# Neighbourhood attention two heads at a time, their score products alternating between the two row halves of the array

## The chip, the cores and the metric

The kernel runs on one core of a Trainium2 chip. The metric is the device time of one execution in microseconds (us); lower is better. The core has five engines that run side by side, each through its own instructions in order: TensorE (PE in the rows; PEld is its weight load) multiplies, VectorE (DVE), ScalarE (ACT) and GpSimd (POOL) work element by element, SyncE (SP) issues transfers. Products are written to PSUM, which has eight banks of 512 float32 columns on 128 partitions.

## The reference, cut to what matters

Two layers, each with four token mixers in parallel on the same normalised input, merged by gates and projected. Inputs are a context stream and a latent stream of 256 tokens each, 1024 channels. The change touches the second mixer, neighbourhood attention, with 8 heads of 64 channels: a latent token reads the 256 context keys and, of the latent grid, the keys in a window of columns, with a learned bias; a context token reads context keys alone (first layer only, the second layer needs no context output).

```python
s_win = jnp.einsum('bqhd,brkhd->bhqrk', qr, kb).astype(jnp.float32) * scale + bias
s_win = jnp.where(col_mask[:, None, :], s_win, -jnp.inf)
s_ctx = jnp.einsum('bqhd,bkhd->bhqk', qr, kc).astype(jnp.float32) * scale
s = jnp.concatenate([s_win.reshape(B, H, GRID_W, n_win), s_ctx], axis=-1)
p = jax.nn.softmax(s, axis=-1).astype(v.dtype)
```

The first mixer, latent attention, also has 8 heads. In this kernel its queries and keys fill 128 rows for each head; those of neighbourhood attention fill 64.

## The kernel before

**Products.** A float32 product is made of three matmuls on the halves of an exact split (high by high, high by low, low by high); `mm3` (L388) issues them into one PSUM bank. A weight piece of 128 x 1024 is loaded into one of three `raw` buffers, split by ScalarE (L423, the high part) and VectorE (L424, the low part; the rows show it at the helper's line L370) and used by TensorE (`pc`, products with channels on the partitions; `pj`, with tokens on the partitions; `br`, of the branches; `wo`, of the output).

**Order.** The program is written out by cooperating tasks. A task yields a time for which it is left aside, or a condition; `drive` (L302) gives TensorE to the first task in order of priority that can go on, on a clock of its own (`self.clock`) that each product advances by a cost. So TensorE's order is fixed by hand, and the table `WAIT` holds how long a step is left aside in each layer. The order on the other engines is made by the scheduler of the framework. Each engine then waits by semaphores for what it needs.

**Attention.** `unit` (L791) does one head's 128 queries: three matmuls into a bank `sc` of the pool `pa` (four banks, which also hold `y` and, in the first layer, `ada`), the bias added to the latent half of the keys (VectorE), the row maximum (VectorE), the exponential and its row sum (ScalarE), the reciprocal and the scaling (VectorE). It is left aside for `WAIT["probs"]`; then come transposes into a bank `pt` of another pool (two banks), and copies. `attention` (L815) goes over the streams, the two heads of a column tile and the two query tiles, and starts a unit as soon as fewer than `UNITS`, 3, are in flight. `values` (L836) multiplies by the values when the four units of a stream are done. Keys are 256 for a context query tile and 512 for a latent one.

**Around it.** `na` (L988) takes the four column tiles of two heads in turn. Head 0 of a tile lies on partitions 0 to 63 of `qs` and `ks`, head 1 on 64 to 127 (L999). At the same time, at a lower priority, the layer's own stream of projections runs: `na_qk` makes the queries and keys, then `gate_list` makes the four chunks of merge gates (`pj`), which need nothing from the attention; after them it waits for the attention to be done (L1448) and goes on to the branch products. The first layer has 32 units (16 with 256 keys, 16 with 512), the second 16 with 512 keys.

Of the kernel before, what the change touches and what calls it, by code (L numbers as in the profile page):

```python
# [12 lines left out]
AF = mybir.ActivationFunctionType  # L13
ALU = mybir.AluOpType
# [49 lines left out]
# chunks whose products come out with channels on the partitions  # L64
# [52 lines left out]
def _pieces(w, k, n):  # L117
    """[.., rows, cols] as [.., (column block, row block), partition, k, n], flat"""
    b, rows, cols = w.shape
    return w.reshape(b, rows // (k * P), k, P, cols // n, n).transpose(0, 4, 1, 3, 2, 5).reshape(b, -1)  # L120


def _layout(x, c, ctx, c_ctx, ada_w, ada_b, pre_g, post_g, w_in, mla_q_norm, mla_w_uq, mla_kv_norm, mla_w_ukv, na_rpb,
# [76 lines left out]
# how long the static order of the tensor engine leaves a task aside after the step of that name, for layers 0 and 1  # L200
# [7 lines left out]
    "norm_step": (1.25, 0.61),  # L208
    "filt_in": (3.1, 4.0),
    "filt_sin1": (6.0, 15.54),  # L210
# [5 lines left out]
    "filt_dft": (0.1, 0.5),  # L216
    "filt_out": (1.82, 4.9),
    "probs": (5.63, 6.4),
    "probs_out": (1.36, 1.13),
# [6 lines left out]
    "mla_k": (0.8, 0.5),  # L226
    "mla_q": (0.25, 0.5),
    "mla_q_out": (1.7, 1.69),
    "na_in": (2.48, 0.97),
# [16 lines left out]
    "gla_keys": (6.0, 6.0),  # L246
# [5 lines left out]
    "merged_step": (0.48, 0.0),  # L252
# [3 lines left out]
UNITS = (3, 3)  # L256
# [7 lines left out]
class Block:  # L264
    """Emits the program as cooperating tasks. A task yields how long it is to be left aside before its next
    instruction of the tensor engine, or a condition; the driver keeps the tensor engine's
    order: the first task that can go on, by priority."""
# [141 lines left out]
    def piece(self, src, k, n, spare=False):  # L409
        """row blocks of (high, low) parts; spare: in the pool s, not in the weights' own"""  # L410
# [21 lines left out]
    def w_tok(self, l, name, c, n=256):  # L432
        """a column block, as function of the row block"""
        return self.rows([self.w_in(l, name, 2 * c + i, 4, n) for i in range(2)])
# [5 lines left out]
    def h_alloc(self, l, s):  # L440
        """layer 0: both streams side by side, four row blocks to a tile; layer 1: a tile for each stream"""
# [5 lines left out]
    def hT(self, s, kt, a, b, n=1):  # L447
        """n row blocks of a stream; a, b may span both streams in layer 0"""
# [5 lines left out]
    def tok(self, w, lhs, nk, s, base):  # L454
        """a stream's two token tiles by 256 columns"""
# [72 lines left out]
    def ada_load(self, l, part, j, half, tiles):  # L528
        """four row blocks, in one tile or in two"""
# [9 lines left out]
    def ada_mm(self, half, w, ps, start, stop):  # L539
        """four row blocks side by side on the columns of the array; each leaves its part of the sum"""  # L540
# [154 lines left out]
    def filters(self, l, loaded=None):  # L695
# [11 lines left out]
        # the hidden layer's high parts on one half of the partitions, its low parts on the other  # L707
# [83 lines left out]
    def unit(self, q, k, nk, bias, pt):  # L791
        nc = self.nc
        ps = self.ps(self.pa, "sc")
        self.mm3(ps[:, :nk], q, k, True, True)
        if bias is not None:
            self.add(nc.vector, ps[:, 256:512], ps[:, 256:512], bias)
        mx, sm, rs = self.t(1, "mx"), self.t(1, "sm"), self.t(1, "rs")
        nc.vector.tensor_reduce(out=mx, in_=ps[:, :nk], axis=AX.X, op=ALU.max, negate=True)  # L798
        p = self.T("p")
        nc.scalar.activation(p[:, :nk], ps[:, :nk], AF.Exp, bias=mx, scale=1.0, accum_out=sm)  # L800
        nc.vector.reciprocal(rs, sm)
        self.ts(p[:, :nk], p[:, :nk], rs, ALU.mult)
        yield self.wait("probs")
        nb = nk // P
        pp = self.ps(self.pt, "pt", (P, 4, P))
        for b in range(nb):
            self.tr(pp[:, b, :], p[:, b * P : b * P + P])
        for b in range(0, nb, 2):
            if b:
                nc.vector.tensor_copy(pt[b // 2], pp[:, b : b + 2, :])  # L810
            else:
                nc.scalar.copy(pt[b // 2], pp[:, b : b + 2, :])
        yield self.wait("probs_out")

    def attention(self, outs, qk, v, bias, ys, g, ct):  # L815
        """two heads: qk(h, t0, nk) gives the lhsT of a query tile and the rhs of its keys"""
        last = None
        for s in outs:
            nk = 256 if s == 0 else 512
            units, pts = [], []  # L820
            for h in range(2):
                pt = [self.T("pt", (P, 2, 256)) for _ in range(nk // 256)]
                for i in range(2):
                    yield lambda: sum(not u.done for u in self.units) < UNITS[self.l]
                    q, k = qk(h, s * 256 + i * P, nk)
                    u = self.spawn(self.unit(q, k, nk, bias[h][:, i, :] if s == 1 and bias is not None else None,
                                             [t[:, :, i * P : i * P + P] for t in pt]), 0)
                    self.units = [w for w in self.units if not w.done] + [u]
                    units.append(u)
                    yield 0  # L830
                pts.append(pt)
# [709 lines left out]
```

## Time and profile before

| | us |
|---|---|
| three runs | 1438.08, 1433.96, 1438.87 (median 1438.08) |
| profiled execution, from its first to its last instruction | 1441.0 |
| TensorE busy in it | 1377.8 (96%) |
| VectorE, ScalarE, GpSimd busy | 894.9, 591.5, 337.2 |
| neighbourhood attention with the projections beside it, first layer | about 690 to 826 |
| the same, second layer | about 1309 to 1391 |

The profile shows no time of the profiled execution other than its span. Start times in the rows are from the start of the span. Matmuls overlap, so a matmul's duration is longer than what it takes from the next one: what a matmul costs is read from the start of one to the start of the next. A row of the timeline may merge several instructions (x3, x6) and carries the shape of the first.

### The profile page before, as it was taken

Reading aid. Unit: us, or ns where it says so; the run is one execution under the profiler, and the core shown is the slowest. Engines: PE = TensorE matmul, PEld = TensorE weight load, DVE = VectorE, ACT = ScalarE, POOL = GpSimd, SP = SyncE. Lnnn points to the kernel's source line nnn. Section 1 sums busy time; section 2 is a strip of 40 time slices with the busy share of each in tenths; the row PEclk is TensorE's granted clock in tenths of the full one; section 3 lists DMA queues with packets and bytes.
Section 4 is the critical chain, followed back from the end, with each engine's and each line's share of the span. In section 5 each row is a group of like instructions: output and inputs, shape, how many; then the busy total and the mean of one; then the engine's idle time right before and its main releaser. Section 6 shows DMA issues by size and latency. Waiting matters only on the chain.

```text
span 1441.0 us, 24777 instructions
## 1 busy us (share of the span) xinstructions
PE 1377.8 (96%) x9852; PEld 1195.6 (83%) x9852; DVE 894.9 (62%) x1638; ACT 591.5 (41%) x1266; POOL 337.2 (23%) x438
## 2 busy tenths in 40 slices
PE   6989999999999999999999999889998999999997
PEld 3867789888997777899768899778888999898796
DVE  4668653575444448664565576867567776767763
ACT  3555453332322242232344433554435445334451
POOL 2423200153230102132011204522104331231120
PEclk8989999999999999999999999999989999999998
DMA  9421222232233432333341352432133256433351
GB/s 376 149 79 52 88 73 92 88 102 89 89 117 117 159 104 88 117 108 127 103 142 63 106 170 67 138 111 87 60 119 118 95 186 203 162 105 133 116 191 58
DMA packets 54308, 171.10 MB, mean 119 GB/s; under 512 B 7342, under 2 KB 10000, under 8 KB 54192
## 3 DMA queue, kind: packets, MB, share of 16 engines
q1 hardware_dynamic: 47904, 153.31, 31.3%
q0 software_dynamic: 5376, 15.90, 3.4%
q8 instruction: 77, 1.26, 0.3%
q10 hardware_dynamic: 912, 0.31, 0.1%
q14 instruction: 39, 0.32, 0.1%
HBM read 163.19 MB, written 6.31 MB: 118 GB/s over the span
## 4 chain that ended last, share of the span: by engine, by line
PE 79%; DVE 8%; DMA 4%; issue 3%; ACT 2%; POOL 2%; DVEq 0%; POOLq 0%; ACTq 0%
PE pj L380 25%; PE pc L380 18%; PE br L380 8%; PE wo L380 4%; PE sc L380 4%; DMA raw<-in_w_in 3%; PE y L380 3%; DVE wl L370 3%; PE pt L394 2%; PE ada L380 2%; PE pa L380 2%; PE go L380 2%; PE yc L380 1%; PE q L380 1%; PE adat L380 1%
## 5 line engine op out<-in xcount | busy, mean ns | idle before, releaser
L370 DVE TENSOR_TENSOR wl<-raw,wh 128x512 fp32r<-128x512 f32 (+1 forms) x416 | 297.7, 750 | 180.7 <-ACT wh L423 175.0
L423 ACT CAST wh<-raw 128x512 fp32r<-128x512 f32 (+1 forms) x416 | 235.9, 616 | 343.5 <-DMA raw<-in_w_in 142.3
L380 PE MATMUL pj<-wh,hh 128*128 128x256 f32 x1024 | 303.6, 297 | 0.0
L380 PE MATMUL pj<-wl,hh 128*128 128x256 f32 x1024 | 290.4, 284 | 0.0
L380 PE MATMUL pj<-wh,hl 128*128 128x256 f32 x1024 | 290.4, 284 | 0.0
L380 PE MATMUL pc<-hh,wh 128*128 128x256 f32 (+1 forms) x688 | 244.8, 356 | 5.4 <-DVE merged L373 1.7
L380 PE MATMUL pc<-hh,wl 128*128 128x256 f32 (+1 forms) x688 | 230.5, 335 | 0.0
L380 PE MATMUL pc<-hl,wh 128*128 128x256 f32 (+1 forms) x688 | 230.4, 335 | 0.0
L380 PEld LDWEIGHTS pj<-wh,hh 128*128 128x128 f32 x1024 | 196.7, 192 | 20.4 <-issue 19.3
L380 PEld LDWEIGHTS pj<-wl,hh 128*128 128x128 f32 x1024 | 197.1, 193 | 2.6 <-issue 1.9
L380 PEld LDWEIGHTS pj<-wh,hl 128*128 128x128 f32 x1024 | 196.8, 192 | 0.0
L380 PEld LDWEIGHTS pc<-hh,wh 128*128 128x128 f32 x688 | 131.8, 192 | 34.5 <-issue 17.8
L380 PEld LDWEIGHTS pc<-hl,wh 128*128 128x128 f32 x688 | 131.8, 192 | 14.0 <-issue 3.4
L380 PEld LDWEIGHTS pc<-hh,wl 128*128 128x128 f32 x688 | 131.6, 191 | 13.5
L380 PE MATMUL br<-wh,gh 128*128 128x256 f32 x384 | 110.3, 287 | 1.7 <-DVE gt L373 1.7
L370 POOL TENSOR_TENSOR gl<-y,gh 128x256 fp32r<-128x256 f32 (+1 forms) x44 | 35.9, 818 | 321.2 <-ACT gh L405 321.2
L380 PE MATMUL br<-wh,gl 128*128 128x256 f32 x384 | 108.7, 283 | 0.0
L380 PE MATMUL br<-wl,gh 128*128 128x256 f32 x384 | 108.6, 283 | 0.0
L800 ACT ACTIVATE p<-sc,mx 128x512 f32<-128x512 f32 (+1 forms) x96 | 59.2, 616 | 67.5 <-DVE mx L798 59.6
L380 PEld LDWEIGHTS br<-wh,gh 128*128 128x128 f32 x384 | 73.6, 192 | 5.7 <-issue 2.9
L380 PEld LDWEIGHTS br<-wh,gl 128*128 128x128 f32 x384 | 73.6, 192 | 0.1
L380 PEld LDWEIGHTS br<-wl,gh 128*128 128x128 f32 x384 | 73.6, 192 | 0.0
(282 smaller groups left out, 2428.6 us busy)
## 6 DMA issues: line engine op xcount, KB each, us to landing
raw<-in_w_in SPq DMA_DIRECT2D x160, 512.0 KB, 3.5
adaw<-in_ada_w SPq DMA_DIRECT2D x44, 512.0 KB, 3.5
raw<-in_w_branch SPq DMA_DIRECT2D x32, 512.0 KB, 3.5
raw<-in_w_out SPq DMA_DIRECT2D x16, 512.0 KB, 3.9
H<-filt POOLq DMA_DIRECT2D x16, 256.0 KB, 3.7
nab<-in_na_bias POOLq DMA_DIRECT2D x16, 256.0 KB, 3.0
raw<-in_w_in SPq DMA_DIRECT2D x8, 448.0 KB, 3.8
x<-in_xin SPq DMA_DIRECT2D x4, 512.0 KB, 5.0
```

What stands on the lines that cost most here:

```text
L370: eng.tensor_tensor(out=out, in0=a, in1=b, op=ALU.subtract)
L380: self.nc.tensor.matmul(out, lhsT, rhs, start=start, stop=stop, skip_group_check=skip)
L394: self.nc.tensor.transpose(out, in_, self.ident)
L423: nc.scalar.copy(hi, raw[:, sl])
L800: nc.scalar.activation(p[:, :nk], ps[:, :nk], AF.Exp, bias=mx, scale=1.0, accum_out=sm)
```

## The change

The unit of attention takes a list of heads. For latent attention the list has one head, with three units in flight as before. For neighbourhood attention it has both heads of a column tile, with two such pairs in flight. The six score matmuls of a pair alternate between head 0 (array rows 0 to 63) and head 1 (rows 64 to 127), each head in its own bank; on the planner's clock they cost half. Then come both heads' bias, maximum and exponential, then both reciprocals and scalings; a pair is left aside for a new time, `probs2`, and then both heads are transposed and copied. The tiles `pt` of both heads are taken before the first unit of a stream, for latent attention too. Seven other entries of the waiting table change a little. The remaining lines of the diff are comments that are removed.

```diff
 WAIT = {
-    "norm_step": (1.25, 0.61),
+    "norm_step": (1.25, 0.52),
-    "filt_sin1": (6.0, 15.54),
+    "filt_sin1": (5.41, 15.54),
-    "filt_dft": (0.1, 0.5),
+    "filt_dft": (0.3, 0.5),
     "probs": (5.63, 6.4),
+    "probs2": (6.22, 7.6),
-    "mla_k": (0.8, 0.5),
+    "mla_k": (0.96, 0.5),
-    "na_in": (2.48, 0.97),
+    "na_in": (2.48, 1.37),
-    "gla_keys": (6.0, 6.0),
+    "gla_keys": (6.49, 6.0),
-    "merged_step": (0.48, 0.0),
+    "merged_step": (0.48, 0),
...
-UNITS = (3, 3)
...
-    def unit(self, q, k, nk, bias, pt):
+    def unit(self, qk, nk, bias, pts):
         nc = self.nc
-        ps = self.ps(self.pa, "sc")
-        self.mm3(ps[:, :nk], q, k, True, True)
-        if bias is not None:
-            self.add(nc.vector, ps[:, 256:512], ps[:, 256:512], bias)
-        mx, sm, rs = self.t(1, "mx"), self.t(1, "sm"), self.t(1, "rs")
-        nc.vector.tensor_reduce(out=mx, in_=ps[:, :nk], axis=AX.X, op=ALU.max, negate=True)
-        p = self.T("p")
-        nc.scalar.activation(p[:, :nk], ps[:, :nk], AF.Exp, bias=mx, scale=1.0, accum_out=sm)
-        nc.vector.reciprocal(rs, sm)
-        self.ts(p[:, :nk], p[:, :nk], rs, ALU.mult)
-        yield self.wait("probs")
+        nh = len(qk)
+        ps = [self.ps(self.pa, "sc") for _ in qk]
+        for i, (a, b) in enumerate(((0, 0), (0, 1), (1, 0))):
+            for h, (q, k) in enumerate(qk):
+                self.mm(ps[h][:, :nk], q[a], k[b], i == 0, i == 2, skip=True, cost=nk / 2400 / nh)
+        ps_, p = [], []
+        for h in range(nh):
+            if bias is not None:
+                self.add(nc.vector, ps[h][:, 256:512], ps[h][:, 256:512], bias[h])
+            mx, sm, rs = self.t(1, "mx"), self.t(1, "sm"), self.t(1, "rs")
+            nc.vector.tensor_reduce(out=mx, in_=ps[h][:, :nk], axis=AX.X, op=ALU.max, negate=True)
+            p.append(self.T("p"))
+            nc.scalar.activation(p[h][:, :nk], ps[h][:, :nk], AF.Exp, bias=mx, scale=1.0, accum_out=sm)
+            ps_.append((sm, rs))
+        for h, (sm, rs) in enumerate(ps_):
+            nc.vector.reciprocal(rs, sm)
+            self.ts(p[h][:, :nk], p[h][:, :nk], rs, ALU.mult)
+        yield self.wait("probs" if nh == 1 else "probs2")
         nb = nk // P
-        pp = self.ps(self.pt, "pt", (P, 4, P))
+        for h in range(nh):
+            pp = self.ps(self.pt, "pt", (P, 4, P))
...
     def attention(self, outs, qk, v, bias, ys, g, ct):
+        groups, most = (((0,), (1,)), 3) if bias is None else (((0, 1),), 2)
         last = None
         for s in outs:
             nk = 256 if s == 0 else 512
-            units, pts = [], []
-            for h in range(2):
-                pt = [self.T("pt", (P, 2, 256)) for _ in range(nk // 256)]
-                for i in range(2):
-                    yield lambda: sum(not u.done for u in self.units) < UNITS[self.l]
-                    q, k = qk(h, s * 256 + i * P, nk)
...
+            units = []
+            pts = [[self.T("pt", (P, 2, 256)) for _ in range(nk // 256)] for h in range(2)]
+            for hs, i in ((hs, i) for hs in groups for i in range(2)):
+                yield lambda: sum(not u.done for u in self.units) < most
+                u = self.spawn(self.unit([qk(h, s * 256 + i * P, nk) for h in hs], nk,
+                                         [bias[h][:, i, :] for h in hs] if s == 1 and bias is not None else None,
+                                         [[t[:, :, i * P : i * P + P] for t in pts[h]] for h in hs]), 0)
+                self.units = [w for w in self.units if not w.done] + [u]
+                units.append(u)
+                yield 0
             last = self.spawn(self.values(units, pts, v, ys, g, ct, s), 0)
```

## Rows read from the trace of the kernel before

**Rows 1.** The page: busy time of the engines, its share of the span, instructions.
```profile
PE 1377.8 (96%) x9852; PEld 1195.6 (83%) x9852; DVE 894.9 (62%) x1638; ACT 591.5 (41%) x1266; POOL 337.2 (23%) x438
```
**Rows 2.** Three stretches: us, PE, PEld, DVE, ACT, POOL, clock, transfers.
```profile
90.00:290.00 200.00, 195.98 (x1290) 164.03 (x1289) 125.23 (x238) 91.07 (x209) 40.69 (x43) 1.00 0.24 79
...
690.00:826.00 136.00, 136.00 (x872) 106.62 (x871) 76.65 (x182) 60.49 (x152) 19.63 (x31) 1.00 0.33 105
1309.00:1391.00 82.00, 80.92 (x596) 69.27 (x595) 55.31 (x119) 39.25 (x91) 12.36 (x18) 1.00 0.36 119
```
**Rows 3.** The last two, score banks alone: us, PE, PEld, DVE, ACT.
```profile
690.00:826.00 136.00, 22.73 (x96) 13.60 (x96) 24.22 (x48) 21.52 (x64) 1.00 0.33 105
1309.00:1391.00 82.00, 14.47 (x48) 7.42 (x48) 17.54 (x32) 12.43 (x32) 1.00 0.36 119
```
**Rows 4.** Chain that ended last: gate products after each layer's last values.
```profile
819.90 6.57 PE pj L380 x53
...
1383.22 7.39 PE pj L380 x60
```
**Rows 5.** Timeline of TensorE, two visits to the scores: start, us, instruction.
```profile
706.72 0.61 PE L380 MATMUL sc<-qk,qk 64*128 64x256 f32 x3
707.26 0.50 PE L380 MATMUL pc<-hh,wh 128*128 128x512 f32 x1
707.60 0.40 PE L380 MATMUL pc<-hl,wh 128*128 128x512 f32 x1
707.83 0.40 PE L380 MATMUL pc<-hh,wl 128*128 128x512 f32 x1
708.16 1.66 PE L380 MATMUL sc<-qk,qk 64*128 64x512 f32 x6
709.75 0.51 PE L380 MATMUL pc<-hh,wh 128*128 128x512 f32 x1
710.09 0.40 PE L380 MATMUL pc<-hl,wh 128*128 128x512 f32 x1
```
**Rows 6.** Timeline of TensorE: first and last score rows of each layer.
```profile
698.01 0.97 PE L380 MATMUL sc<-qk,qk 64*128 64x256 f32 x9
...
807.38 0.96 PE L380 MATMUL sc<-qk,qk 64*128 64x512 f32 x3
...
1311.36 0.49 PE L380 MATMUL sc<-qk,qk 64*128 64x512 f32 x1 [0.17 <-ACT qk L984]
...
1370.99 0.96 PE L380 MATMUL sc<-qk,qk 64*128 64x512 f32 x3
```
**Rows 7.** Groups of matmuls by shape, 765.1 to 766.0 us.
```profile
L380 PE MATMUL sc<-qk,qk 64*128 64x512 f32 x3 | 1.0, 426 | 0.0
L380 PE MATMUL sc<-qk,qk 64*128 64x256 f32 x3 | 0.6, 311 | 0.0
```
**Rows 8.** Timeline of TensorE: that visit, then one unit with 512 keys.
```profile
765.14 0.97 PE L380 MATMUL sc<-qk,qk 64*128 64x256 f32 x6
...
738.89 0.97 PE L380 MATMUL sc<-qk,qk 64*128 64x512 f32 x3
```
**Rows 9.** Groups by line: VectorE in the second layer's stretch, ScalarE in the first's.
```profile
L370 DVE TENSOR_TENSOR wl<-raw,wh 128x512 fp32r<-128x512 f32 x28 | 19.6, 729 | 12.6 <-ACT wh L423 12.6
L798 DVE TENSOR_REDUCE mx<-sc 128x1 f32<-128x512 f32 x16 | 10.9, 684 | 0.2
...
L800 ACT ACTIVATE p<-sc,mx 128x512 f32<-128x512 f32 x16 | 11.0, 689 | 11.2 <-DVE mx L798 8.8 <-issue 1.5 <-ACT p L800 0.9
```
**Rows 10.** Timeline, two visits of two 512-key units: ScalarE's last exponential, VectorE's last scalings.
```profile
714.25 0.68 ACT L800 ACTIVATE p<-sc,mx 128x512 f32<-128x512 f32 x1
...
715.33 0.49 DVE L377 TENSOR_SCALAR p<-p,rs 128x512 f32<-128x512 f32 x1
...
1334.41 0.49 DVE L377 TENSOR_SCALAR p<-p,rs 128x512 f32<-128x512 f32 x1
```
**Rows 11.** Timeline of TensorE: the scores of the second of these visits.
```profile
1325.53 1.82 PE L380 MATMUL sc<-qk,qk 64*128 64x512 f32 x6
```

More of the change, by code (lines that the diff above doesn't have):

```diff
@@ L788, in ytiles @@
         return ([self.F("gh", F32R, "gh") for _ in range(4)], [self.F("gl", F32R, "gl") for _ in range(4)])
-    def unit(self, q, k, nk, bias, pt):
+    def unit(self, qk, nk, bias, pts):
         nc = self.nc
-        ps = self.ps(self.pa, "sc")
-        self.mm3(ps[:, :nk], q, k, True, True)
-        if bias is not None:
-            self.add(nc.vector, ps[:, 256:512], ps[:, 256:512], bias)
-        mx, sm, rs = self.t(1, "mx"), self.t(1, "sm"), self.t(1, "rs")
-        nc.vector.tensor_reduce(out=mx, in_=ps[:, :nk], axis=AX.X, op=ALU.max, negate=True)
-        p = self.T("p")
-        nc.scalar.activation(p[:, :nk], ps[:, :nk], AF.Exp, bias=mx, scale=1.0, accum_out=sm)
-        nc.vector.reciprocal(rs, sm)
-        self.ts(p[:, :nk], p[:, :nk], rs, ALU.mult)
-        yield self.wait("probs")
-        nb = nk // P
-        pp = self.ps(self.pt, "pt", (P, 4, P))
[L806 to L812, printed above, removed]
+        nh = len(qk)
[16 more added lines that the diff above has]
+        yield self.wait("probs" if nh == 1 else "probs2")
+        nb = nk // P
+        for h in range(nh):
+            pp = self.ps(self.pt, "pt", (P, 4, P))
+            for b in range(nb):
+                self.tr(pp[:, b, :], p[h][:, b * P : b * P + P])
+            for b in range(0, nb, 2):
+                if b:
+                    nc.vector.tensor_copy(pts[h][b // 2], pp[:, b : b + 2, :])
+                else:
+                    nc.scalar.copy(pts[h][b // 2], pp[:, b : b + 2, :])
@@ L819, in attention @@
             nk = 256 if s == 0 else 512
-            units, pts = [], []
-            for h in range(2):
-                pt = [self.T("pt", (P, 2, 256)) for _ in range(nk // 256)]
-                for i in range(2):
-                    yield lambda: sum(not u.done for u in self.units) < UNITS[self.l]
-                    q, k = qk(h, s * 256 + i * P, nk)
[L826 to L831, printed above, removed]
+            units = []
[8 more added lines that the diff above has]
+                yield 0
             last = self.spawn(self.values(units, pts, v, ys, g, ct, s), 0)
```

## The prediction

> **What bounds the kernel now.** The page comes first: TensorE is busy for 1377.8 us of the span of 1441.0 us, far ahead of VectorE's 894.9 us [rows 1]. An average proves nothing about one stage, so the view of busy time by stretch comes second. While neighbourhood attention runs beside its projections, TensorE is busy for all 136 us of the first layer's stretch and for 80.9 of 82 us in the second layer's; VectorE has 76.7 and 55.3 us there, ScalarE 60.5 and 39.3, and the granted clock is full [rows 2]. The chain that ended last says whether this work is really what the end waits for: after the last values of each layer it still runs through 6.6 and 7.4 us of gate products [rows 4]. These need nothing of the attention. So the attention's latency is covered, and what these stretches take is the sum of TensorE's work. What TensorE is spared here comes off the end, as long as it isn't made to wait for something else.
>
> **The scores as they are.** The instructions on score banks are 96 and 48 matmuls [rows 3], that is 32 and 16 units of three. The timeline gives their price from start to start. A matmul with 512 columns follows its like after 0.23 us (707.60 to 707.83) [rows 5]. From the last `pc` before the visit at 708.16 us (707.83) to the second one after it (710.09) is 2.26 us and holds eight such products, 1.84 us; 0.42 us is lost on entering and leaving the 64-row form [rows 5]. Three matmuls with 256 columns take 0.54 us to the next product (706.72 to 707.26) [rows 5]. About half of the loss, 0.2 us, lies inside that time, which leaves 0.34 us of streaming (my estimate from those rows). In the whole timeline I count 25 visits in the first layer and 13 in the second, one of which is shown as two rows [rows 6]. I charge 0.41 us for each, since visits next to values or transposes lose a little less or more.
>
> Before, then: 32 units x 0.69 us (22.1) + 16 x 0.34 us (5.4) + 38 visits x 0.41 us (15.6) = 43.1 us. From this come off 0.7 us for two visits that already overlap, one of which is the key to this change. It is the visit at 765.14 us: it holds three matmuls with 512 columns and three with 256 [rows 7], the second head of one stream and the first head of the next. Its modelled 0.97 us is that of three with 512 columns alone at 738.89 us [rows 8]. So three products of one row half cost nothing beside three of the other half. The other is the one of nine matmuls at 698.01 us, 0.97 us where a single unit has 0.61: two more units for 0.36 us, about the time of one [rows 5, 6]. This makes 42.4 us before.
>
> **The change, part by part.** *Alternation and pairing.* After, there are 24 pairs: 16 with 512 keys at 3 x 0.23 = 0.69 us of streaming, 8 with 256 keys at 0.34 us, and at most 24 visits at 0.41 us: 11.0 + 2.7 + 9.8 = 23.5 us. The difference is -18.9 us. The bounds: if the halves don't overlap, streaming stays at 27.5 us and only 14 visits (5.7 us) less the two overlaps (0.7 us) are won, -5.0 us; if the two pairs of a stream go out together in 8 of the 12 groups, 8 visits less remain, 3.3 us more, -22.2 us. I keep a visit for each pair, because values and gates come between them on the planner's clock.
>
> Here a rule speaks against the full gain. The Trainium skill (TensorE: Matmul & The Clock Gate, Part 3: Packing small matmuls) measured 3.07 times the speed for four row tiles, so not four. If two tiles lost as large a share, they would give 1.53 times; streaming would be 18.0 us in place of 13.7, and the change would win 4.3 us less, 1428.3 us, inside the forecast's own range (an estimate from that page). The visit at 765.14 us shows no such loss [rows 7, 8], and I go by it.
>
> *Softmax of two heads.* The work on VectorE and ScalarE is the same; its latency is new. The transposes of a pair stand in TensorE's order 6.22 us (first layer) or 7.6 us (second) after its scores on the planner's clock, which charges 0.213 us where 0.23 us pass, so some 6.7 and 8.2 us on the chip. The nearest rows are visits in which two units with 512 keys went out together: the second scaling ends at 715.82 us, 6.0 us after the scores' end at 709.82 us [rows 5, 10], and in the second layer at 1334.90 us, 7.55 us after 1327.35 us [rows 10, 11]. That is just inside. A late one makes TensorE stand, and with it all products queued behind the transposes. Below, the price is nothing; above, one more pair of low-part splits ahead in VectorE's queue, 2 x 0.73 us [rows 9], less the slack of 0.65 us, so 0.8 us for each of 24 pairs, 19 us. The two rows lie nearer to nothing: I take 0.1 us each, +2.4 us.
>
> *Banks.* Two pairs hold four score banks, all of pool `pa`; `y` needs a fifth between the pairs, 12 times (once for each stream of a column tile). Before, three units and `y` just fitted. A bank is held until its exponential ends, in the visit above at 714.93 us, 5.1 us after the scores [rows 5, 10]; so the price lies between nothing and 12 x 5.1 = 61 us. But the values and the transposes that come between two pairs spread them out: the second pair of a group follows the first by a `y` of 0.9 or 1.8 us and 0.9 us of transposes on the planner's clock, and the first group's delay persists into the next. What is left is a short wait in the groups at the start of a tile; I take 0.2 us on average, +2.4 us. No row of before shows such a wait, so this is the least certain term.
>
> *The rest.* Transposes, copies and values keep their number. The earlier `pt` tiles touch latent attention too, but their buffers are written only by copies, and TensorE is busy 196 of 200 us in its first stretch [rows 2]; I set nothing, and if that cover is gone a buffer that is late costs one copy's wait. The seven table entries move steps by 0.6 us at most, some before work that TensorE fills anyway: nothing, within 3 us either way, since every order after them shifts. The weight pieces keep up: ScalarE and VectorE have 44 and 56% of the first stretch [rows 2].
>
> Sum: -18.9 + 2.4 + 2.4 = -14.1 us. The profiled span, 1441.0 us, lies 2.9 us above the median of the runs, 1438.08 us, and nothing around it is shown; on that execution the sum gives 1426.9 us. I put the difference on the median: 1424.0 us.
>
> **The rivals.** *The halves don't overlap in this form* (three accumulating steps that alternate, each with a weight load). Then -5.0 + 4.8: 1437.9 us. Against it stand [rows 7, 8]; for it, that there the overlap came between units, never step by step.
>
> *Banks or softmax take most of it.* If TensorE stands 0.55 us for each pair, 13.2 us, the gain is 18.9 - 13.2 = 5.7 us: 1432.4 us. For it: VectorE is at 67% in the second layer's stretch [rows 2], and a pair asks for its work in a burst. Beside this stands the Trainium skill (TensorEngine Tiling (Array Packing), Gotcha 1: PSUM Pressure): row tiles need different banks, so the pressure rises. No row of before shows its price.
>
> *Slower: the pair's softmax comes late every time.* Here it is one mechanism: TensorE reaches the transposes of the second head before its scaling has ended. At 18.9 / 24 = 0.79 us for each pair the gain is gone; at 1.1 us (1.5 low-part splits of 0.73 us ahead) it is 26.4 - 18.9 = +7.5 us: 1445.6 us. Against it stand the two visits of [rows 10].
>
> **How the numbers follow.** Forecast 70%, banks or softmax 14%, no overlap 8%, slower 8%. About 0.3%, 4.3 us, is what a measurement can tell from no change. The forecast lies wholly below that line and so does most of the second case (11 of its 14%): faster 81%. Same: the rest of it and most of no overlap, 10%. Slower: 9%. The likeliest case alone reaches from 1416 us (visits that merge, -22.2, and no waits) to 1430 us. The range for 8 in 10 takes in the second case and ends just short of no overlap: 1414 to 1437 us.
>
> **What would show it.** Right: score visits hold six matmuls, two starting within some ns of each other, and a pair with 512 keys takes about 0.9 us to the next product; busy time on score banks falls from 37.2 us [rows 3] to under 25 us; the stretches of [rows 2] become some 10 and 6 us shorter, and gates still end them. Wrong: scores that start 0.23 us apart; transposes that wait for `p`, or scores that wait for an exponential, by half a microsecond each; the last values coming after the last gate; or latent attention, which shouldn't move, growing by more than 3 us.

## The result, and the profile after

| | median of the runs | lowest to highest | runs |
|---|---|---|---|
| before | 1436.38 us | 1433.96 to 1438.87 | 4 |
| after | 1423.28 us | 1420.96 to 1426.96 | 4 |

The ratio is 0.9913, with a 95% interval from 0.9893 to 0.9934: 0.9% faster, 13.1 us by the medians, where -14.1 us and 1424.0 us were forecast. The profiled execution of after took 1426.96 us with a span of 1425.2 us. The change does what it says, but the -13.1 us are not put together quite as the prediction had them: one term that it priced at nothing cost 3.3 us, and one of its waits did not show by itself.

The page of after, busy time of the engines (beside [rows 1]): TensorE has the same 9852 instructions and 18.0 us less of busy time.

```profile
PE 1359.8 (95%) x9852; PEld 1187.0 (83%) x9852; DVE 889.0 (62%) x1638; ACT 591.3 (41%) x1266; POOL 339.7 (24%) x438
```

Busy time of after in the two stretches of neighbourhood attention (columns as in [rows 2]), for all work and then for the score banks alone (as in [rows 3]). They end earlier now, so the windows were moved; the second one holds 653 matmuls where it held 596, so there only the score rows compare like with like. Score banks fall from 37.2 us of busy TensorE time to 12.9 + 8.2 = 21.1 us for the same 96 + 48 matmuls; the forecast was under 25. VectorE and ScalarE do what they did. In the first layer TensorE is no longer busy all the time: 127.0 of 130 us.

```profile
690.00:820.00 130.00, 127.01 (x872) 100.28 (x871) 76.01 (x182) 58.27 (x149) 21.73 (x31) 1.00 0.34 111
1296.00:1378.00 82.00, 80.86 (x653) 72.57 (x652) 56.44 (x123) 40.14 (x93) 13.76 (x21) 1.00 0.45 148
...
690.00:820.00 130.00, 12.93 (x96) 7.33 (x96) 21.98 (x48) 20.25 (x64) 1.00 0.34 111
1296.00:1378.00 82.00, 8.21 (x48) 4.14 (x48) 15.74 (x32) 12.01 (x32) 1.00 0.45 148
```

The timeline of TensorE in after (start, us, instruction, in brackets the idle time before it and what ended it) answers to [rows 5] and shows what was won and what was lost.

```profile
700.37 0.97 PE L380 MATMUL sc<-qk,qk 64*128 64x256 f32 x12
701.27 0.50 PE L380 MATMUL pc<-hh,wh 128*128 128x512 f32 x1
...
711.72 0.96 PE L380 MATMUL sc<-qk,qk 64*128 64x512 f32 x6
712.62 1.08 PE L380 MATMUL y<-pt,na_v 128*64 128x256 f32 x8
713.63 0.49 PE L380 MATMUL sc<-qk,qk 64*128 64x512 f32 x1
715.00 0.96 PE L380 MATMUL sc<-qk,qk 64*128 64x512 f32 x5 [0.88 <-ACT p L806]
715.89 0.64 PE L380 MATMUL ada<-adaw,sv 128*32 128x256 f32 x8
...
741.94 0.59 PE L380 MATMUL adat<-rows,par 128*2 128x256 f32 x2
...
743.95 0.60 PE L394 MATMUL pt<-ident,p 128*128 128x128 f32 x4
745.48 0.66 PE L394 MATMUL pt<-ident,p 128*128 128x128 f32 x4 [0.92 <-DVE pt L819]
...
1314.89 1.03 PE L394 MATMUL pt<-ident,p 128*128 128x128 f32 x8
1316.51 1.09 PE L394 MATMUL pt<-ident,p 128*128 128x128 f32 x8 [0.58 <-DVE pt L819]
```

*What was won.* The visit at 711.72 us holds a pair with 512 keys, six matmuls, and the next product starts 0.90 us later; the six of [rows 5] at 708.16 us took 1.59 us. One by one, the six start at 711.722, 711.726, 712.060, 712.063, 712.296 and 712.299 us: each product of the second head 3 or 4 ns behind that of the first. The visit at 700.37 us shows that two pairs can go out together: twelve matmuls with 256 keys in 0.90 us.

*What was lost.* The next pair finds its second bank taken. Its first matmul starts at 713.63 us, the other five at 715.00 us, after an exponential (line 806) has let a bank go; until the next instruction at 715.89 us this visit takes 2.26 us where the one before took 0.90. The second kind of wait stands at 745.48 us: the transposes of the second head come 1.53 us after those of the first, where four transposes otherwise take 0.36 us (from 711.38 to 711.74 us in e4). VectorE's timeline in after says why.

```profile
743.61 0.49 DVE L377 TENSOR_SCALAR p<-p,rs 128x512 f32<-128x512 f32 x1
...
744.28 0.49 DVE L377 TENSOR_SCALAR p<-p,rs 128x512 f32<-128x512 f32 x1
745.00 0.42 DVE L819 COPY pt<-pt 128x256 f32<-128x256 f32 x1 [0.23 <-ACT pt L821]
...
747.89 0.41 DVE L367 TENSOR_TENSOR gb<-adat,gb 2x256 f32<-2x256 f32 x1
...
1314.23 1.29 DVE L370 TENSOR_TENSOR wl<-raw,wh 128x512 fp32r<-128x512 f32 x2
1315.44 0.69 DVE L373 SCALAR_TENSOR_TENSOR qk<-pc,qk 128x512 fp32r<-128x512 f32 x1
1316.04 0.75 DVE L819 COPY pt<-pt 128x256 f32<-128x256 f32 x2
```

The pool `pt` has two PSUM banks, and the `adat` products of the adaptive norm (741.94 us) hold one of them until VectorE reads it at 747.89 us. Both heads' transposes go through the other: the second head's wait until VectorE has copied the first's out, at 745.42 us. Its own probabilities were scaled at 744.77 us, so a free bank would have shortened this wait and not removed it. In the second layer the pair's eight transposes (1314.89 us) fill both banks, and the next pair's eight wait for copies that stand in VectorE's queue behind two low-part splits and a `qk`.

Gates still end both stretches: the chain of after, answering to [rows 4], runs through 13.2 and 7.1 us of gate products behind the last values `y`.

```profile
807.73 1.88 PE y L380 x16
809.60 13.15 PE pj L380 x108
...
1363.42 1.88 PE y L380 x16
1365.30 7.10 PE pj L380 x58
```

For an account of each stretch I add up, over the timeline, the time from each TensorE instruction's start to the next one's, by what it writes. The first layer's stretch runs from the 481st branch product (`br`) to the 577th (from 671.1 to 826.4 us in before), the second layer's from the 961st to the 1057th. Idle time falls to the instruction before it, and what is lost on entering and leaving the 64-row form falls partly to `sc`, partly to the projections.

| us | before | after | e1 | e2 | e3 | e4 | e7 | e8 | e11 |
|---|---|---|---|---|---|---|---|---|---|
| first layer, all | 155.3 | 149.0 | 148.3 | 157.1 | 146.3 | 145.5 | 152.8 | 154.5 | 146.5 |
| scores `sc` | 21.0 | 12.8 | 12.8 | 20.3 | 12.8 | 11.6 | 18.6 | 16.8 | 13.1 |
| transposes `pt` | 10.3 | 13.1 | 12.6 | 12.6 | 11.1 | 10.3 | 10.3 | 11.6 | 11.1 |
| `pc` and `pj` | 96.4 | 94.9 | 94.7 | 95.4 | 94.8 | 95.4 | 96.4 | 97.8 | 94.8 |
| second layer, all | 101.0 | 94.2 | 94.4 | 98.1 | 96.9 | 93.1 | 100.6 | 97.2 | 94.2 |
| scores `sc` | 14.0 | 7.7 | 8.0 | 11.7 | 8.6 | 7.6 | 13.6 | 8.8 | 7.7 |
| transposes `pt` | 7.1 | 7.6 | 7.6 | 7.6 | 10.0 | 6.3 | 7.1 | 8.7 | 7.6 |
| `pc` and `pj` | 60.9 | 59.8 | 59.8 | 59.8 | 59.2 | 59.8 | 60.9 | 60.7 | 59.8 |

The two stretches are 6.3 and 6.9 us shorter, 13.1 us together, as much as the medians differ. That the two agree to a tenth is in part luck, since shifts outside the stretches cancel: the first layer's Hyena takes 3.0 us more (227.7 us in before, 230.7 us in e5, a second profile of the changed kernel), and the ways from the first branch product to the 97th and from the 577th to the 673rd take 1.1 and 2.2 us less (28.1 to 27.0 us, 13.7 to 11.5 us). These sums repeat: three profiles of the changed kernel give 149.0, 149.2 and 149.0 us, and 94.2, 94.1 and 94.2 us. The profiled spans differ by more, 15.8 us (1441.0 and 1425.2), because other stretches shift by some microseconds from one kernel, and from one execution, to the next. One of these shifts comes with the change: the way from the 384th branch product to the 385th, the first layer's Hyena, is 227.7 us in before and 232.5 us in after. About 1.8 us of the difference goes with a short stretch of this execution in which TensorE's granted clock was half, which e5's profile has not (e9 to e12 below).

### The profile page after: what moved, and what is told of

It is laid out like the page before. It is cut to its first block, busy times and chain, and to the rows that moved or that the text cites. A ratio compares the mean times of both kernels' runs of the same rounds, so it can differ in the third digit from the quotient of the medians.

```text
span 1425.2 us, 24774 instructions
## 1 busy us (share of the span) xinstructions
PE 1359.8 (95%) x9852; PEld 1187.0 (83%) x9852; DVE 889.0 (62%) x1638; ACT 591.3 (41%) x1266; POOL 339.7 (24%) x438
## 4 chain that ended last, share of the span: by engine, by line
PE 44%; DVE 7%; issue 3%; DMA 2%; ACT 1%; POOL 1%; DVEq 0%; POOLq 0%; ACTq 0%
PE pj L380 14%; PE pc L380 9%; PE br L380 5%; PE wo L380 3%; DVE wl L370 2%; PE sc L380 2%; PE y L380 2%; DMA raw<-in_w_in 2%; PE pt L394 2%; PE pa L380 1%; PE yc L380 1%; DMA raw<-in_w_out 1%; PE go L380 1%; ACT wh L423 0%; PE q L380 0%
## 5 line engine op out<-in xcount | busy, mean ns | idle before, releaser
L380 PE MATMUL pc<-hl,wh 128*128 128x256 f32 (+1 forms) x688 | 230.9, 336 | 0.0
L380 PEld LDWEIGHTS pc<-hl,wh 128*128 128x128 f32 x688 | 132.6, 193 | 14.1 <-issue 3.1
```

The source lines that it names most:

```text
L380: self.nc.tensor.matmul(out, lhsT, rhs, start=start, stop=stop, skip_group_check=skip)
```

## The experiments

Twelve experiments were made with ten kernels, in three groups. Each group had its own runs of before on the same chip: medians of 1434.06 us (13 runs) for e1 to e4, 1435.85 us (23 runs) for e5 to e8, 1436.42 us (11 runs) for e9 to e12. Ratios are against those. The first group has no run of the changed kernel; e1 to e4 are held against its ratios in the others, 0.9913 to 0.9931. The theory: the gain is the overlap of the two row halves, together with the fewer visits; what it falls short by is TensorE waiting for PSUM banks. Its rivals: it is the alternation step by step; it is the pairing alone, without overlap; it is the table's new entries.

**e1: head 0's three products, then head 1's three.** The alternation goes, the pair stays.

```diff
-        for i, (a, b) in enumerate(((0, 0), (0, 1), (1, 0))):
-            for h, (q, k) in enumerate(qk):
+        for h, (q, k) in enumerate(qk):
+            for i, (a, b) in enumerate(((0, 0), (0, 1), (1, 0))):
```

> The changed kernel with the six score matmuls of a pair in another order: head 0's three, then head 1's three. Everything else is the same, the planner's cost too. Theory A: the two row halves take their matmuls independently of each other, so what brings the overlap is that both halves are in one visit, not the alternation. Then a 512-key pair still takes about 0.9 us to the next product and the time stays within 3 us of the changed kernel's 1423 us. Rival B: TensorE starts matmuls in their order, so only head 0's third and head 1's first overlap. Then a 512-key pair takes about 1.35 us, a 256-key pair 0.78 us, and the time is 16 x 0.46 + 8 x 0.23 = 9 us longer, about 1432 us.

Measured: 1424.72 us, ratio 0.9934 [0.9908, 0.9960]. The timeline of TensorE in e1:

```profile
708.41 0.97 PE L380 MATMUL sc<-qk,qk 64*128 64x512 f32 x6
709.32 1.08 PE L380 MATMUL y<-pt,na_v 128*64 128x256 f32 x8
710.33 0.96 PE L380 MATMUL sc<-qk,qk 64*128 64x512 f32 x3
711.50 0.96 PE L380 MATMUL sc<-qk,qk 64*128 64x512 f32 x3 [0.21 <-ACT p L806]
```

Six matmuls, issued head by head, still take 0.91 us to the next product, and start in twos, 10 ns apart (708.413 and 708.423). The alternation is not needed: what counts is that products of both halves stand beside each other with nothing between. The rival, that TensorE starts matmuls in their order, is excluded: the semaphore update that each head's third product carries stands, in the trace, on the fifth and the sixth start, so head 0's third product started only behind head 1's second, which stands two places after it in the program. The two rows from 710.33 us show the one difference: when the second bank is late, head 0's three products are done before the wait and only head 1's come after it.

**e2: pairs of one head.** Two query tiles of the same head make a pair, so both are in the same row half; the number of pairs, banks and steps stays.

```diff
-        groups, most = (((0,), (1,)), 3) if bias is None else (((0, 1),), 2)
+        groups, most = ((((0, 0),), ((0, 1),), ((1, 0),), ((1, 1),)), 3) if bias is None else ((((0, 0), (0, 1)), ((1, 0), (1, 1))), 2)
...
-            for hs, i in ((hs, i) for hs in groups for i in range(2)):
+            for hs in groups:
```

> The changed kernel with other pairs: the two query tiles of one head in place of the two heads of one query tile, so that both members of a pair lie on the same row half; they still alternate between two banks and leave together, and the planner still charges half. Theory: the overlap of the halves carries most of the gain. Then a 512-key pair takes 1.59 us and a 256-key pair 0.9 us to the next product, the scores cost 16 x 0.69 + 8 x 0.34 = 13.7 us more, and the time is about 1437 us, that of the kernel before. Rival: pairing (fewer visits, two heads' softmax in one burst) carries it. Then the time stays within 3 us of 1423 us.

Measured: 1437.47 us (10 runs), ratio 1.0027 [1.0009, 1.0044]. The timeline of TensorE in e2, at the visit that answers to 711.72 us of after:

```profile
707.63 1.65 PE L380 MATMUL sc<-qk,qk 64*128 64x512 f32 x6
709.21 1.08 PE L380 MATMUL y<-pt,na_v 128*64 128x256 f32 x8
```

1.58 us instead of 0.90; the starts lie 0.23 to 0.34 us apart, as in before. Scores cost 20.3 + 11.7 = 32.0 us in the account, 11.5 more than after. So without the overlap nothing is won: fewer visits save 3.0 us on scores (35.0 to 32.0) and 2.1 us on the projections (157.3 to 155.2), the transposes lose 2.8 us (17.4 to 20.2) as they do in after, and both stretches together are 1.2 us shorter than before's. That the whole is slightly slower than before fits the first layer's Hyena, which takes 232.1 us here (227.7 in before), in part by a stretch of half clock (e9 to e12).

**e3: the table as it was.** Six entries back at their old values; the new one, `probs2`, stays. (The seventh of the diff, `merged_step`, is 0 in both kernels.)

```diff
-    "norm_step": (1.25, 0.52),
+    "norm_step": (1.25, 0.61),
-    "filt_sin1": (5.41, 15.54),
+    "filt_sin1": (6.0, 15.54),
-    "filt_dft": (0.3, 0.5),
+    "filt_dft": (0.1, 0.5),
-    "mla_k": (0.96, 0.5),
+    "mla_k": (0.8, 0.5),
-    "na_in": (2.48, 1.37),
+    "na_in": (2.48, 0.97),
-    "gla_keys": (6.49, 6.0),
+    "gla_keys": (6.0, 6.0),
```

> The changed kernel with the six other changed entries of the waiting table set back to their values of before; probs2 stays. Theory: these entries only shift the order elsewhere, by 3 us at most either way, and the score visits stay as they are: 1420 to 1426 us. Rival: the entries carry part of the gain, and the time grows by 5 us or more, to 1428 us or above.

Measured: 1420.74 us, ratio 0.9906 [0.9889, 0.9922]. The gain does not come from the entries. The account shows that they are not without effect, though: the first layer's stretch is 2.7 us shorter than after's, the second layer's 2.7 us longer (its transposes 10.0 us, where after has 7.6).

**e4: the second pair of a column tile 3 us later.** Meant to take the bank waits away: the first two pairs no longer go out together.

```diff
-                yield 0
+                yield 3.0 if bias is not None and s == outs[0] and i == 0 else 0
```

> The changed kernel in which, at the first stream of each column tile, the second pair of neighbourhood attention starts 3 us later on the planner's clock. Theory: the waits of scores for a bank (0.88 us at 715.0 us in the trace after) and of transposes for a bank (0.9 and 0.6 us) come from two pairs that start back to back; spread out, they go, and the time falls by 2 to 4 us, to about 1420 us. Rival: the waits only move to other visits, as the pairs are in step again one stream later, and the time stays within 2 us of 1423 us.

Measured: 1423.46 us, ratio 0.9929 [0.9914, 0.9943]. In both stretches the trace shows no wait of TensorE any more, transposes are back at 10.3 and 6.3 us, and the two stretches are 4.6 us shorter than after's. The time does not show it: its ratio is no lower than the changed kernel's 0.9913 to 0.9931. Part of it can be seen going: right behind the first layer's stretch, the waits of TensorE in e4 have a row that the changed kernel's second profile (e5) has not, a branch product that waits for a gate.

```profile
PE br L380 <- DVE gt L373: 1.3, 1, 1.3
```

**e5: the changed kernel again**, as the partner of the next three.

> The changed kernel again, as the yardstick for the three others on the same chip: 0.991 of the kernel before. Any theory expects the same.

Measured: 1424.81 us (6 runs), ratio 0.9931 [0.9912, 0.9950].

**e6: e4's delay with e3's table.**

```diff
-                yield 0
+                yield 3.0 if bias is not None and s == outs[0] and i == 0 else 0
...
-    "na_in": (2.48, 1.37),
+    "na_in": (2.48, 0.97),
...
```

> The changed kernel with both earlier edits together: the second pair of a column tile starts 3 us later on the planner's clock, and the six other table entries are those of before. Theory: the bank waits were worth about 4.6 us in the two attention stretches of the trace (149.0 + 94.2 us with the change, 145.5 + 93.1 us spread out), and the old entries do no harm elsewhere, so the time is 3 to 6 us below the changed kernel on the same chip, ratio 0.987 to 0.989. Rival: what the stretches win is given back elsewhere as the order shifts, and the time stays within 2 us of it.

Measured: 1423.86 us (6 runs), ratio 0.9922 [0.9905, 0.9939]: 1 us from e5, which these runs cannot tell from nothing, and the expected 0.987 to 0.989 was missed. The stretches are 144.7 and 95.8 us, 2.8 us less than e5's in sum. Taking the waits away pays in the stretch and, as in e4, little of it reaches the end; a gate that comes 1.5 us late is again the one row of waits from 690 to 825 us. The clock is a second part: the mean granted clock of TensorE over a whole run is 0.985 in the mean of e4's four runs, 0.9855 in that of e6's six, and 0.987 in those of after's four and e5's six. In the 23 runs of before in this group, the seven at 0.985 or less (0.984 in the mean) have a median of 1438.67 us, the eight at 0.990 or more (0.991) one of 1433.80 us; by these the difference here is worth about 1 us (my estimate). Whether the later pair itself lowers the clock was not tested.

**e7: before, with its units in another order.** Before's single units, started query tile by query tile, so that the heads alternate; nothing is paired. Where two units go out together they are now of different halves.

```diff
-            for h in range(2):
-                pt = [self.T("pt", (P, 2, 256)) for _ in range(nk // 256)]
-                for i in range(2):
+            pts = [[self.T("pt", (P, 2, 256)) for _ in range(nk // 256)] for h in range(2)]
+            for x, y in ((x, y) for x in range(2) for y in range(2)):
+                    h, i = (x, y) if bias is None else (y, x)
+                    pt = pts[h]
```

> The kernel before, with one part of the change alone: units of one head each, three in flight, but started query tile by query tile, so that the two heads of a tile follow one another (both heads' pt tiles are taken before the first unit). Theory: the overlap needs both halves in one visit; single units mostly come 1 to 6 us apart, so only the few visits with two or three units gain, 1 to 4 us in all, ratio 0.997 to 1. Rival: alternating the heads is enough, and most of the 13 us comes, ratio 0.991 to 0.993.

Measured: 1431.69 us (12 runs), ratio 0.9980 [0.9963, 0.9996], as expected. The timeline of TensorE in e7, at a visit of two units:

```profile
703.19 0.97 PE L380 MATMUL sc<-qk,qk 64*128 64x512 f32 x6
704.09 0.50 PE L380 MATMUL pc<-hh,wh 128*128 128x512 f32 x1
```

0.90 us, as in a pair, where [rows 5] has 1.59. But 25 + 13 visits remain, most of them with one unit, and scores fall only by 2.4 + 0.4 us. Order alone wins 3 to 4 us (0.2% of 1435.85 us, 4.2 us by the medians); the pair is what makes every visit hold both halves.

**e8: the pair's products in two visits.** After the first step of each pair the planner may put other work between. The same overlap, 42 visits instead of 22.

```diff
                 self.mm(ps[h][:, :nk], q[a], k[b], i == 0, i == 2, skip=True, cost=nk / 2400 / nh)
+            if nh == 2 and i == 0:
+                yield 0.3
```

> The changed kernel with a doubled cost: after the first two score matmuls of a pair, the pair is left aside for 0.3 us on the planner's clock, so that other products come between them and the other four, and nearly every pair takes two visits. Theory: entering and leaving the 64-row form costs about 0.41 us a visit; 20 to 24 more visits add 8 to 10 us to the changed kernel, ratio about 0.998 of the kernel before. Rival: the loss on entering and leaving is only how the trace draws pipelined matmuls, and the time stays within 3 us of the changed kernel.

Measured: 1436.60 us (12 runs), ratio 1.0007 [0.9994, 1.0021]: 11.8 us over e5, the whole gain. The rival is excluded. The price of a visit is read best where nothing else disturbs: a pair with 512 keys among gate products, in one visit in after's timeline,

```profile
758.78 0.28 PE L380 MATMUL pj<-wh,hl 128*128 128x256 f32 x1
759.00 0.96 PE L380 MATMUL sc<-qk,qk 64*128 64x512 f32 x6
759.89 0.39 PE L380 MATMUL pj<-wh,hh 128*128 128x256 f32 x1
760.11 0.28 PE L380 MATMUL pj<-wl,hh 128*128 128x256 f32 x1
```

and in two visits, of two and of four matmuls, in e8's:

```profile
766.69 0.28 PE L380 MATMUL pj<-wh,hl 128*128 128x256 f32 x1
766.90 0.49 PE L380 MATMUL sc<-qk,qk 64*128 64x512 f32 x2
767.32 0.39 PE L380 MATMUL pj<-wh,hh 128*128 128x256 f32 x1
767.55 0.28 PE L380 MATMUL pj<-wl,hh 128*128 128x256 f32 x1
...
768.02 0.28 PE L380 MATMUL pj<-wh,hl 128*128 128x256 f32 x1
768.23 0.73 PE L380 MATMUL sc<-qk,qk 64*128 64x512 f32 x4
768.90 0.39 PE L380 MATMUL pj<-wh,hh 128*128 128x256 f32 x1
769.12 0.28 PE L380 MATMUL pj<-wl,hh 128*128 128x256 f32 x1
```

From the last `pj` before a visit to the second one after it, the pair takes 1.33 us in one visit and 0.86 + 1.10 us in two. Of the two, 0.24 us are two more gate products at 0.12 us, so the second visit costs 0.39 us; the prediction had 0.41 us from [rows 5].

The account is rougher. Scores rise by 5.1 us over e5's 20.4 and the projections by 3.8 us over 154.7: 8.9 us for 20 more visits, 0.45 us each. But some 2.8 us of this (my estimate from the trace) is something else: a wait of TensorE behind scores is longer here (2.02 us idle before 716.93 us, 0.87 us in e5), and behind it the granted clock is at half for a stretch, in which `pc` products start 0.43 us apart and not 0.23. Busy time of that stretch, columns as in [rows 2]:

```profile
717.60:721.00 3.40, 3.40 (x10) 2.27 (x11) 3.06 (x9) 0.90 (x3) 0.00 (x0) 0.51 0.79 269
```

Without these, about 0.3 us a visit is left in the account. So more visits explain some 6 to 8 of the 11.8 us; the rest was not separated.

**e9 to e12: what the table's entries do.** Left open by e3 was the first layer's Hyena: 225.3 to 227.7 us in the four kernels so far with the old entries (before, e3, e6, e7), 230.6 to 232.5 us in the six with the new. e9 is e3 again, e10 the changed kernel again; e11 is e3 with `na_in` left at its new value; e12 is the changed kernel with the two entries of the Hyena filters put back.

```diff
# e11, beside e3
-    "na_in": (2.48, 0.97),
+    "na_in": (2.48, 1.37),
# e12, beside the changed kernel
-    "filt_sin1": (5.41, 15.54),
+    "filt_sin1": (6.0, 15.54),
-    "filt_dft": (0.3, 0.5),
+    "filt_dft": (0.1, 0.5),
```

> The changed kernel with six entries of the table back at their values of before (the pair's own new entry stays), against the changed kernel in the same group of runs. Theory (entries carry a loss of their own): the four profiles with the old entries (before, the first run of this kernel, the staggered one with the old table, the swapped order) spend 225.3 to 227.7 us between the 384th and the 385th branch product, in the first layer's Hyena; the six with the new entries 230.6 to 232.5 us, with waits of yc for VectorE of 2.3 us. So some 5 us come back there, some 2.8 us in the first layer's attention stretch (146.3 for 149.1), while 1.6 us are lost ahead of Hyena and 2.7 us in the second layer's attention (96.9 for 94.1): about 3 to 4 us faster than the changed kernel, some 1421 us, and the Hyena stretch at 225 to 227 us again. Rival (the entries carry nothing, what is late there is made up elsewhere): within 1 us of the changed kernel.

> The changed kernel once more, as the partner of the three others: some 1424 us, ratio to before 0.991 to 0.993, Hyena stretch of the first layer 230 to 232 us, attention stretches 149 and 94 us, as in its two earlier profiles. Both theories expect the same.

> Five of the six entries back, na_in of the second layer left at its new 1.37. Theory (entries cost or win by stage): the second layer's attention stretch is 94 us as in the changed kernel and not 96.9, all else as with the old entries: some 6 us faster than the changed kernel, near 1418 us, ratio to before 0.987 to 0.989. Rival (shifts are made up elsewhere): no further from the changed kernel than the kernel with all six back, within 1 us of it.

> Only the two entries of the Hyena filters in the first layer back (filt_sin1 6.0, filt_dft 0.1). Theory (these two make the 5 us): the first layer's Hyena stretch falls from 231 to 225 to 228 us, yc's waits of 2.3 us are gone, and the time is 3 to 5 us below the changed kernel. Rival (other entries, or the shift of all orders after any of them): the stretch stays at 230 us or more, and the time within 1 us of the changed kernel.

| | median | lowest to highest | ratio to before | Hyena, first layer | stretches |
|---|---|---|---|---|---|
| e9, six entries back | 1423.17 us (6 runs) | 1417.46 to 1424.70 | 0.9895 [0.9871, 0.9918] | 225.7 us | 146.5, 96.8 us |
| e10, changed kernel | 1424.81 us (6 runs) | 1422.82 to 1436.46 | 0.9926 [0.9897, 0.9956] | 235.9 us | 149.0, 94.2 us |
| e11, all back but `na_in` | 1418.18 us (5 runs) | 1416.15 to 1420.68 | 0.9876 [0.9854, 0.9899] | 226.1 us | 146.5, 94.2 us |
| e12, two back | 1424.01 us (6 runs) | 1423.03 to 1428.68 | 0.9914 [0.9894, 0.9934] | 233.5 us | 149.0, 94.2 us |

e11 came out as expected: none of its runs reaches the lowest of e10's, and its median is 6.6 us below (ratio of the medians 0.9953). It beats both kernels. e9 lies 1.6 us below e10 where 3 to 4 us were expected, with runs that overlap; neither case is settled by that pair alone. e12's theory fell: the filters' entries do not make Hyena longer. Of the other five, `norm_step` and `na_in` changed in the second layer alone, which leaves `mla_k` and `gla_keys` for the first layer's Hyena; they were not tried one by one. The profiled run of e10 is the one that took 1436.46 us, at the lowest mean granted clock of the six (0.980); its Hyena is longer than in the other profiles of this kernel, its attention stretches are not. Its trace shows two waits of TensorE in Hyena with a stretch of half clock (1.2 of 2.4 GHz) behind each, from 506.0 and from 639.1 us: the row of the first wait, then the busy time of the stretch behind it.

```profile
505.56 0.36 PE L394 MATMUL hyt<-ident,cv 128*128 128x128 f32 x1 [1.68 <-DVE cv L373]
...
506.00:509.40 3.40, 3.40 (x17) 2.22 (x10) 0.42 (x1) 1.12 (x2) 0.00 (x0) 0.50 0.59 194
```

This sorts the profiles with the new entries. Those without such a stretch in Hyena take 230.6 to 230.9 us there (e1, e4, e5), those with one 232.1 to 233.5 us (after, e2, e8, e12), e10 with two 235.9 us. With the old `mla_k` and `gla_keys` no profile has one: 225.3 to 227.7 us. So in Hyena the entries cost some 3 to 6 us by themselves, and 1 to 5 us more in an execution in which the clock drops.

What TensorE waits for from 440 to 660 us, first in after (us in all, times, longest):

```profile
PE hyt L394 <- DVE cv L373: 1.5, 1, 1.5
PE yc L380 <- DVE wi L367: 1.3, 1, 1.3
PE yc L380 <- DVE wr L367: 1.0, 1, 1.0
PE pc L380 <- DVE zg L373: 0.8, 1, 0.8
PE yv L380 <- DVE wr L367: 0.4, 1, 0.4
```

and then in e11:

```profile
PE yv L380 <- DVE wr L367: 0.8, 1, 0.8
PE hyt L394 <- DVE cv L373: 0.3, 1, 0.3
PE yc L380 <- DVE wi L367: 0.2, 1, 0.2
```

The waits are 5.0 us and 1.3 us (before: 2.6 us): TensorE comes to Hyena's steps while VectorE is not yet through, at other places for each order.

## Why the prediction was right, step by step

*The bound.* Right. Work taken off TensorE in the two stretches came off the end, 13.1 us in the account and 13.1 us by the medians, and gates still end both stretches. Elsewhere the shifts cancel, so the equal sums are in part luck. Latent attention did not grow: up to the first branch product, before takes 242.6 us, after 240.6 and, in e5's profile, 242.4 us.

*Scores, -18.9 us.* Right. In the account, scores fall by 14.5 us (35.0 to 20.5) and the projections, which bear part of the entering and leaving, by 2.6 us (157.3 to 154.7): -17.1 us. This still holds the bank waits (below, 1.9 us); without them it is -19.0 us. Of its parts, overlap (e2: scores cost 11.5 us more without it) and price of a visit (e8: 0.39 us for 0.41) are shown; the visits are 15 + 7 = 22, where 24 were charged, since two pairs went out together now and then. The loss that the Trainium skill's figure for four row tiles would give two (TensorE: Matmul & The Clock Gate, Part 3: Packing small matmuls) is not in this trace: a pair's starts keep the distance of 0.23 to 0.34 us that one head's have in e2, where nothing overlaps.

*Banks, +2.4 us.* Right in size, and in place: 2.26 - 0.90 = 1.4 us at 713.63 us, in a group at the start of a tile, and 0.5 us in the second layer (from 1321.01 to 1322.41 us, 1.40 us for 0.90), together +1.9 us. Not 12 small waits, but two larger ones. It is what the Trainium skill warns of under PSUM pressure (TensorEngine Tiling (Array Packing), Gotcha 1), and here it costs 1.9 us beside a gain of 13.1.

*Softmax of two heads, +2.4 us.* Not seen by itself. No row of waits names the probabilities; at 745.48 us they would have been late by 0.46 us (744.77 less 744.31), but the bank came later still.

*Transposes "keep their number", priced at nothing.* This step was wrong, by +3.3 us (10.3 to 13.1 and 7.1 to 7.6). The number is kept, their spacing is not: a pair sends twice as many into the two banks of `pt` at once, and these come free only by copies in VectorE's and ScalarE's queues, or are held by `adat`. I counted banks for `pa` and not for `pt`. That it is this and no change of the transposes themselves is shown by e4: spread out, they cost 10.3 and 6.3 us. (Of the 1.2 us lost at 745.48 us, 0.46 us would have gone to the probabilities anyway.) Two errors thus nearly cancel: lateness charged at +2.4 us to the probabilities arose as +3.3 us at the banks behind them.

*Table entries, nothing within 3 us.* The size holds for the six together: e9 lies 1.6 us below e10, and e3, in another group, has 0.9906 where the changed kernel has 0.9913 to 0.9931. But it is a sum of opposite parts. `na_in` wins 2.7 us in the second layer (e9 and e11: 96.8 and 94.2 us; the medians differ by 5.0 us), the other five lose 6.6 us (e11 and e10), by the account 2.5 us in the first layer's attention and 4.6 us in Hyena (226.1 us in e11, 230.7 us in e5). With the old table the pairing alone wins 13.3 us in both groups (1434.06 less 1420.74, 1436.42 less 1423.17), as much as the changed kernel's 13.1; with `na_in` as its only companion, 18.2 us (1436.42 less 1418.18).

*Stretches "10 and 6 us shorter".* 6.3 and 6.9. The first layer's falls short by its transposes (2.8 us), its bank wait (1.4 us), and eight more `ada` products that the new order brings into it (0.6 us; e3, with the old table, has 40 as before, the changed kernel 48).

*Sum.* -19.0 + 1.9 + 3.3 + 0.6 = -13.2 us, against -13.1 us of the stretches and of the medians. Of the rivals, no overlap is excluded for this kernel by the starts 3 or 4 ns apart, and its price by e2. The slower case did not come. "Banks or softmax take most of it" was right in kind and too large in size: 5.2 us of waits, not 13.2. Where e4's and e6's shorter stretches go is only partly settled: 1.3 and 1.5 us show up as late gates, and about 1 us goes with the lower granted clock of their runs.

## What to carry to other kernels

When two operands lie in different row halves of the array, see that their products reach TensorE's queue with nothing between; the order within that visit matters little (e1), a second visit costs 0.39 us (e8), and the same pairing within one half wins nothing (e2). Work that is bunched asks for everything behind it in a bunch too: count the PSUM banks of each later step, those of the transposes as those of the scores, and who else holds them. In an order made by a planner, an edit's own entries should be timed apart from the edit: here five of them took back 6.6 us.

## What the runs showed of the hardware that was not expected

Products of the two row halves overlap fully even when they are issued three and three (e1: starts 10 ns apart), across units that know nothing of each other (e7), and in a run of twelve (after, 700.37 us: 0.90 us). The prediction had seen overlap between units only and did not know whether a step by step alternation would keep it; it does. In e1 and e7 the products start in another order than the program has them: the third of the head that comes first starts behind the second of the other (e1: at 708.98 us, 10 ns before the last of the six).

A wait of TensorE can cost more than its own length. In after, e2, e8, e10 and e12 the granted clock fell to half (1.2 of 2.4 GHz) within 0.1 to 1.6 us after the end of a wait of 1.3 to 1.7 us in Hyena. It did not always: e1, e4 and e5 have such waits and full clock behind them.
